# A two-block fp32 transformer kernel on one core: 128-column first weights, a moved memory projection, and a final norm that shares the feed-forward's space

## The chip, the core and the metric

The kernel runs on one core of one Trainium2 chip. The metric is the device time of one execution in microseconds (us), the median of three runs.

## The reference

One sequence of 256 tokens with 1024 features passes two blocks. What matters here:

```python
h = rmsnorm(x, norm_mix[layer])              # x * rsqrt(mean(x*x) + eps) * gain
mix = nsa_attention(h, ...)                  # layer 0; its projections are h @ w_in
x = x + mix
x = x + swiglu(rmsnorm(x, norm_ffn[layer]), ffn_w_up[layer], ffn_w_down[layer])
...                                          # layer 1: dilated attention, then the same swiglu
x = rmsnorm(x, final_norm)                   # end of the first block
...
x = x + 0.5 * swiglu_ffn(rms_norm(x, ffn1_norm[l]), ffn1_w_in[l], ffn1_w_out[l])
mem_kv = rms_norm(mem, mem_norm[l]) @ w_mem_kv[l]      # needs no x at all
...                                          # three-branch mixer, ffn2
x = rms_norm(x, final_norm[l])
```

Inside `nsa_attention` the keys and values of 32-token windows are "compressed": 16 shifted copies of the projected k and v, plus a position term, go through a two-layer perceptron with gelu.

## The kernel before

Activations are held transposed, as eight tiles `x0` to `x7` of 128 features by 256 tokens. The stages run in the order nsa, ffn0, dil (dilated attention), ffn1, ffn1_2 (the first feed-forward of the second block, with the first block's final norm folded in), mix, ffn2_2 and the last norm.

Every projection is made in full fp32 accuracy from halves: a weight tile is loaded as `raw` (1 MB, four buffers, SP's queue, L177), ScalarE copies it to a rounded half `wh` (L190) and VectorE makes the rest `wl` (L191); the input is split in the same way into `xh` (ScalarE, L279) and `xl` (VectorE, L280). `mm3` (L226) then issues three matmuls for each of the eight 128-row pieces, wh·xh (L231), wl·xh and wh·xl, so a projection of 128 columns is 24 matmuls of 256 columns. In the order that TensorE runs them, L231, L232 and L233 are the three products of a piece. A weight pair has four buffers (`wsplit`), and PSUM banks go by the tags mm, sc, tr and ov.

A norm is folded into its projection. The projections take x times the gain, not divided by the root mean square; the squares are summed aside (ScalarE L290 to L295 makes them, POOL adds them at L296, TensorE sums over the features at L304, POOL raises to the power -1/2 at L315, TensorE spreads the row over partitions at L327), and the result is multiplied by R = 1/rms when it leaves PSUM. `norm_twice` (L359) does two norms in a row from one set of x, so ffn1_2 can start from the x that ffn1 leaves: `r1` is the first norm's factor, `r2` the second's, made from `ss2` (L379 to L386).

The program is recorded in Python, and a scheduler then sets a fixed order for each engine from priorities: `high_priority(offset=AHEAD)` pulls work forward by 400 steps, `-BEHIND` pushes it back. On the chip each engine runs its list strictly in order, and a wait holds back all that stands behind it.

Three places matter. At the **start**, `nsa` (L527) norms x, projects the window keys and values (`windows`, L567; the first two weight tiles, `first`, are loaded in `body` with x), and starts the compression (`hidden`, L603, and `compression`, L609, whose gelu is at L613). In the **middle**, `body` calls `mem_project` (L1085) between ffn1 and ffn1_2: four projections of the memory, which need nothing of x. `between` (L1370) is called by `ffn` (L392) before its third and fifth pair of hidden tiles and does `mem_keys` and `s5_prepare`, small VectorE work. At the **end**, `final` (L854) opens a pool of its own for the eight results `res`, scales x by the gain into them (L866), and multiplies by the norm's factor (L874, L876) before the output transfers.

Of the kernel before, what the change touches and what calls it, by code (L numbers as in the profile page):

```python
# [11 lines left out]
F32 = mybir.dt.float32  # L12
F32R = mybir.dt.float32r
AF = mybir.ActivationFunctionType
ALU = mybir.AluOpType
# [3 lines left out]
P = 128  # L19
S = 256  # L20
D = 1024
# [3 lines left out]
EPS = 1e-6  # L25
BIG = 1e30
AHEAD = 400
BEHIND = 100
GAP = 20
WARM = 16  # L30
NU = 384
# [92 lines left out]
class Builder:  # L124
# [221 lines left out]
    def norm_all(self, xs, gains, split=False):  # L346
# [9 lines left out]
            R, r = self.rstd(acc, split)  # L356
        return X, R, r

    def norm_twice(self, pool, xs, first, second):  # L359

        nc = self.nc
        gg = pool.tile([P, KD], F32, name="gg")
        o1, o2 = VOFF[first], VOFF[second]
        nc.vector.tensor_tensor(gg, self.gains[:, o1:o1 + KD], self.gains[:, o2:o2 + KD], ALU.mult)
        acc, acc2 = self.sq_begin(), pool.tile([P, 2, S], F32, name="sqacc2")
        X = []
        with self.tc.high_priority(offset=AHEAD):  # L370
            for k in range(KD):
                X.append(self.gsplit(xs[k], gg[:, k:k + 1], k))
                self.sq_add(acc, xs[k], k)
                self.sq_add(acc2, xs[k], k, self.gain(first, k))
            ps = self.bank("ov")
            self.sq_sum(ps, acc)
            self.sq_sum(ps[:, 2:4], acc2)
            ss2 = pool.tile([P, 2], F32, name="ss2")
            nc.vector.tensor_copy(ss2, ps[:, 2:4])  # L379
            r1 = self.rms(ps[:, 0:2])  # L380
            for _ in range(2):
                for tb in range(2):
                    nc.vector.tensor_tensor(ss2[:, tb:tb + 1], ss2[:, tb:tb + 1], r1[tb], ALU.mult)
            r2 = self.rms(ss2)
            for tb in range(2):
                nc.vector.tensor_tensor(r2[tb], r2[tb], r1[tb], ALU.mult)  # L386
            R = self.rows_kept(r2)
        self.scale(xs, first, self.rows(r1))
        return X, R


    def ffn(self, xs, gain, w_up, w_down, factor, between=None, after=None, skew=0, split=False):  # L392
        nc, tc = self.nc, self.tc
        with tc.tile_pool(name=self.n("hid"), bufs=1) as hp:
            if skew:
                self.pad(hp, skew)
            if after:
                X, R = self.norm_twice(hp, xs, after, gain)
            else:
                (X,), R, _ = self.norm_all(xs, [gain], split)  # L400
            H = []
            self.hid = hp
            for mp in range(KF // 2):
                if mp in (2, 4) and between:
                    between(mp)
                ua = self.units(w_up, D, mp * 256)
                ub = self.units(w_up, D, FF + mp * 256)
                for c in range(2):
                    k = 2 * mp + c
                    pa = self.proj(next(ua), X)  # L410
                    pb = self.proj(next(ub), X)
                    a = hp.tile([P, S], F32, tag="fa", name=self.n("fa"), bufs=2)
                    nc.vector.tensor_tensor(a, pa, R, ALU.mult)
                    b = hp.tile([P, S], F32, tag="fb", name=self.n("fb"), bufs=2)
                    nc.vector.tensor_tensor(b, pb, R, ALU.mult)
                    nc.scalar.activation(a, a, AF.Silu)
                    nc.vector.tensor_tensor(b, a, b, ALU.mult)
                    h = hp.tile([P, S], F32R, name=self.n("hh"), tag=f"hh{k}")
                    l = hp.tile([P, S], F32R, name=self.n("hl"), tag=f"hl{k}")
                    nc.scalar.activation(h, b, AF.Copy)  # L420
                    nc.vector.tensor_tensor(l, b, h.bitcast(F32), ALU.subtract)
                    H.append((h, l))
            self.out_proj(xs, w_down, FF, H, factor)

    def out_proj(self, xs, w, K, X, factor):
        nc = self.nc
# [100 lines left out]
    def nsa(self, xs, first):  # L527
        nc, tc, A = self.nc, self.tc, self.A
        w = A["a_w_in"]
        ukc = itertools.chain(*first)  # L530
        (X,), R, r = self.norm_all(xs, ["norm_mix0"], True)
        with tc.high_priority(offset=-BEHIND):
            self.bias_rows()
        with ExitStack() as es:
# [29 lines left out]

            blks, kcs = [], []

            def windows(wi, units):  # L567
                nm = "kv"[wi]
                if wi == 0:
                    kcs.append(cp.tile([P, 2, 2, S], F32, name="kcv", tag="kcv"))  # L570
                kc = kcs[0][:, wi]
                for mt, u in enumerate(units):
                    self.evac_k(kc[:, mt, :], self.proj(u, X), R)
                blk = cp.tile([P, 16, 60], F32, name="blk" + nm)
                blks.append(blk)
                for gp in range(2):
                    for j2 in range(2):
                        pe = self.v(f"pe_{nm}{j2}", 16)[64 * gp:64 * gp + 64]
                        for half in range(2):
                            src = kc[64 * gp:64 * gp + 64, :, 16 * half:16 * half + 240]  # L580
                            src = src.rearrange("p m (n c j) -> p j c m n", c=8, j=2)[:, j2]
                            dst = blk[64 * j2:64 * j2 + 64, 8 * half:8 * half + 8, 30 * gp:30 * gp + 30]
                            dst = dst.rearrange("p c (m n) -> p c m n", m=2)
                            pb = pe[:, 8 * half:8 * half + 8].unsqueeze(2).unsqueeze(3).to_broadcast([64, 8, 2, 15])
                            (nc.vector if half else nc.gpsimd).tensor_tensor(dst, src, pb, ALU.add)
# [139 lines left out]
                nc.tensor.matmul(Op, Vc[:, g, 2 * j:2 * j + 2, :].rearrange("p i d -> p (i d)"), st["pc"], start=False, stop=True, skip_group_check=True)  # L725
                O.append(self.split_act(Op, "o", 2 * g + j, flip=True))

            windows(0, ukc)
            windows(1, self.units(w, D, 1280))
            keys(0, self.units(w, D, 1536))  # L730
            queries(0)
            keys(1, self.units(w, D, 2048))
# [121 lines left out]
    def final(self, xs, gain):  # L854

        nc = self.nc
        acc = self.sq_begin()
        pool = self.ctx.enter_context(self.tc.tile_pool(name="res", bufs=1))
        res = [pool.tile([P, S], F32, name=f"res{k}") for k in range(KD)]
        Rs = pool.tile([P, S], F32, name="Rs")  # L860
        v = pool.tile([P, 2], F32, name="fv")
        r = pool.tile([P, 2], F32, name="fr")
        with self.tc.high_priority(offset=AHEAD):
            for k in range(KD):
                self.sq_add(acc, xs[k], k, split=True)
# [11 lines left out]
        return res[2:] + res[:2], [*range(2, KD), 0, 1]  # L877

    def scale(self, xs, gain, R):
        for k in range(KD):  # L880
# [458 lines left out]
def body(tc, A, out, stages=None):  # L1339
    stages = stages or STAGES  # L1340
    with ExitStack() as ctx:
        b = Builder(ctx, tc, A)
        nc = b.nc
        xs, first, order = [], [], range(KD)
# [6 lines left out]
        b.rest()  # L1351
        if "nsa" not in stages:
            b.bias_rows()
        late = None
        for s in stages:
# [7 lines left out]
                b.dilated(xs)  # L1363
            elif s == "ffn1":
                b.ffn(xs, "norm_ffn1", A["ffn_w_up1"], A["ffn_w_down1"], 1.0, lambda mp: b.mem_norm(late, mp), skew=352)
                b.mem_project(late)
            elif s == "fin1" and "ffn1_2" not in stages:
                b.final(xs, "final_norm")
            elif s == "ffn1_2":
                def between(mp):  # L1370
                    if mp == 4:
                        return
                    b.vec2 = b.hid.tile([P, 640], F32, name="vec2")[:, :NVEC - NSOON]
                    nc.sync.dma_start(b.vec2, A["vec"][:, NSOON:])
                    b.mem_keys(late)
                    b.s5_prepare(late)
                b.ffn(xs, "ffn1_norm_2", A["ffn1_w_in_2"], A["ffn1_w_out_2"], 0.5, between, "final_norm" if "fin1" in stages else None, skew=288)
            elif s == "mix":
                b.mixer(xs)
            elif s == "ffn2_2":  # L1380
                b.ffn(xs, "ffn2_norm_2", A["ffn2_w_in_2"], A["ffn2_w_out_2"], 0.5, skew=352, split=True)
            elif s == "fin2":
                xs, order = b.final(xs, "final_norm_2")
        for i, (k, x) in enumerate(zip(order, xs)):
            (nc.scalar if i % 2 else nc.sync).dma_start(out[k * P:(k + 1) * P, :], x)


def _pack(I):
# [74 lines left out]
```

## Time and profile before

| what | value |
|---|---|
| three runs | 1338.96, 1335.37 and 1334.37 us |
| median | 1335.37 us |
| profiled execution | 1339.51 us, of which 1337.7 us is the span |
| granted TensorE clock, mean | 0.994 of full |
| busy share of the span | TensorE 98%, VectorE 74%, ScalarE 56%, POOL 15% |

The profiled execution stands 4.14 us above the median. The span is the time from its first to its last instruction on the chip, and 1.8 us of the execution lies around it. TensorE is busy nearly all the time, so what can be won lies in the few places where it is not, or where it runs at the lower of its two clock levels.

### The profile page before, as it was taken

What the parts mean: (1) busy time and instruction counts of PE and PEld (TensorE: products, weight loads), DVE (VectorE), ACT (ScalarE), POOL (GpSimd) and SP (SyncE); (2) the same over time, 40 slices, a digit from 0 to 9 for tenths busy, and PEclk for the clock granted to TensorE, in tenths of its full rate; (3) what the DMA queues carried; (4) which work ended last, traced back from release to release, by engine and by line L of the source; (5) the groups of instructions that cost most, each with busy time, mean ns of one, the idle gap of its engine ahead of it and who ended that gap; (6) DMA issues with size and microseconds to landing.
All of it is one profiled execution on the core that took longest, in us unless ns stands there. A gap on an engine that the chain in (4) does not pass through costs nothing.

```text
span 1337.7 us, 27509 instructions
## 1 busy us (share of the span) xinstructions
PE 1310.3 (98%) x10924; PEld 1245.5 (93%) x10924; DVE 996.5 (74%) x2105; ACT 748.2 (56%) x1422; POOL 196.7 (15%) x244
## 2 busy tenths in 40 slices
PE   9899999999999999999999999999999999999996
PEld 8786999999999887999999999999988879999996
DVE  7899677766797663886855998956699887777752
ACT  5678555555668776754545454544334665555542
POOL 3300100001310000400011332101032044000011
PEclk9999999999999999999999999999999999999998
DMA  9742266646866350665557466755744254566460
GB/s 285 250 151 72 94 205 199 197 144 209 248 204 185 100 143 9 208 195 190 182 174 243 136 200 208 242 180 170 245 154 149 80 174 158 192 196 199 162 198 32
DMA packets 227264, 232.77 MB, mean 174 GB/s; under 512 B 5960, under 2 KB 221328, under 8 KB 227136
## 3 DMA queue, kind: packets, MB, share of 16 engines
q1 hardware_dynamic: 222960, 225.62, 53.0%
q10 hardware_dynamic: 4176, 5.40, 1.2%
q8 instruction: 86, 1.41, 0.4%
q14 instruction: 42, 0.34, 0.1%
HBM read 226.69 MB, written 4.30 MB: 173 GB/s over the span
## 4 chain that ended last, share of the span: by engine, by line
PE 55%; DVE 5%; DMA 1%; issue 1%; ACT 1%; POOL 0%; DVEq 0%; POOLq 0%; ACTq 0%
PE mm L231 7%; PE mm L232 7%; PE mm L233 7%; PE tr L231 4%; PE tr L233 4%; PE tr L232 4%; PE sc L232 4%; PE sc L231 4%; PE sc L233 4%; PE ov L233 2%; PE ov L231 2%; PE ov L232 2%; DVE wl L191 2%; PE ov L493 1%; DMA rot_scratch<-CS 1%
## 5 line engine op out<-in xcount | busy, mean ns | idle before, releaser
L190 ACT ACTIVATE wh<-raw 128x1024 fp32r<-128x1024 f32 (+2 forms) x405 | 417.8, 1036 | 422.9 <-PE mm L232 132.5
L191 DVE TENSOR_TENSOR wl<-raw,wh 128x1024 fp32r<-128x1024 f32 (+2 forms) x405 | 485.1, 1201 | 161.3 <-ACT wh L190 156.8
L231 PE MATMUL mm<-xh,wh 128*128 128x256 f32 x952 | 270.8, 284 | 0.0
L232 PE MATMUL mm<-xl,wh 128*128 128x256 f32 x952 | 267.7, 281 | 1.0 <-DVE xl L280 1.0
L233 PE MATMUL mm<-xh,wl 128*128 128x256 f32 x952 | 267.1, 281 | 1.1 <-DVE wl L191 1.1
L231 PEld LDWEIGHTS mm<-xh,wh 128*128 128x128 f32 x952 | 179.4, 188 | 6.2 <-issue 4.7
L232 PEld LDWEIGHTS mm<-xl,wh 128*128 128x128 f32 x952 | 179.4, 188 | 5.7 <-issue 3.7
L233 PEld LDWEIGHTS mm<-xh,wl 128*128 128x128 f32 x952 | 179.1, 188 | 3.2 <-issue 1.5
L296 POOL TENSOR_TENSOR sqacc<-sqacc,sq 128x256 f32<-128x256 f32 x60 | 57.0, 953 | 536.5 <-ACT sq L295 272.0
L233 PE MATMUL sc<-xh,wl 128*128 128x256 f32 x464 | 129.6, 279 | 0.0
L231 PE MATMUL sc<-xh,wh 128*128 128x256 f32 x464 | 129.5, 279 | 0.0
L232 PE MATMUL sc<-xl,wh 128*128 128x256 f32 x464 | 129.5, 279 | 0.0
L233 PE MATMUL tr<-xh,wl 128*128 128x256 f32 x440 | 123.0, 280 | 3.5 <-DVE wl L191 3.5
L231 PE MATMUL tr<-xh,wh 128*128 128x256 f32 x440 | 123.0, 280 | 0.0
L232 PE MATMUL tr<-xl,wh 128*128 128x256 f32 x440 | 122.8, 279 | 0.0
L233 PEld LDWEIGHTS sc<-xh,wl 128*128 128x128 f32 x464 | 88.0, 190 | 0.1
L231 PEld LDWEIGHTS sc<-xh,wh 128*128 128x128 f32 x464 | 88.0, 190 | 0.0
L232 PEld LDWEIGHTS sc<-xl,wh 128*128 128x128 f32 x464 | 87.9, 189 | 0.0
L233 PEld LDWEIGHTS tr<-xh,wl 128*128 128x128 f32 x440 | 83.5, 190 | 3.9 <-DVE wl L191 3.9
L231 PEld LDWEIGHTS tr<-xh,wh 128*128 128x128 f32 x440 | 83.5, 190 | 0.1
L232 PEld LDWEIGHTS tr<-xl,wh 128*128 128x128 f32 x440 | 83.4, 189 | 0.1
L233 PE MATMUL ov<-xh,wl 128*128 128x256 f32 x224 | 62.2, 278 | 0.2 <-DVE wl L191 0.2
(483 smaller groups left out, 3395.5 us busy)
## 6 DMA issues: line engine op xcount, KB each, us to landing
raw<-in_ffn_w_up_dram SPq DMA_DIRECT2D x44, 1024.0 KB, 5.4
raw<-in_ffn_w_in_dram SPq DMA_DIRECT2D x44, 1024.0 KB, 5.3
raw<-in_w_in_dram SPq DMA_DIRECT2D x17, 1024.0 KB, 5.3
raw<-in_ffn_w_down_dram SPq DMA_DIRECT2D x16, 1024.0 KB, 5.2
raw<-in_ffn_w_out_dram SPq DMA_DIRECT2D x16, 1024.0 KB, 5.1
raw<-in_b_w_q_dram SPq DMA_DIRECT2D x12, 1024.0 KB, 5.2
raw<-in_a_w_in_dram SPq DMA_DIRECT2D x8, 1024.0 KB, 8.3
bt<-u_scratch SPq DMA_DIRECT2D x28, 256.0 KB, 4.7
```

The source lines that it names most:

```text
L190: nc.scalar.activation(hv, v, AF.Copy)
L191: nc.vector.tensor_tensor(lv, v, hv.bitcast(F32), ALU.subtract)
L231: nc.tensor.matmul(ps, sh, mh, start=(i == 0), stop=False)
L232: nc.tensor.matmul(ps, sh, ml, start=False, stop=False)
L233: nc.tensor.matmul(ps, sl, mh, start=False, stop=(i == n - 1))
L296: nc.gpsimd.tensor_tensor(acc[:, 0], acc[:, 0], s, ALU.add)
L493: nc.tensor.matmul(O[64 * i:64 * i + 64, q0:q1], V[kb], pt[:, c0:c0 + q1 - q0], start=(start and kb == 0), stop=(stop and kb == 1), skip_g ...
```

## The change

At the start, the value windows' weights are loaded like the key windows', as 128-column tiles, right behind x; `rest()` (constants and small vectors) moves behind them. All eight x are split first, and the squares are made only then: `norm_begin` gives the squares a scale `one` that is computed from the last `xl`. The four window projections are recorded ahead of the norm's factor, and held in PSUM until it is there. `BEHIND` grows from 100 to 400, which is used for the position-bias rows.

In the middle, `mem_project` moves from ahead of ffn1_2 to its third pair of hidden tiles, and `mem_keys`, `s5_prepare` and their load to the fifth. `norm_twice` hands back its last steps, and `ffn` records them between the first projections.

At the end, `final` runs inside the last feed-forward's pool and takes its tiles from there, and the output transfers are issued in it.

```diff
-BEHIND = 100
+BEHIND = 400
...
+    def norm_begin(self, xs, gain):
+        acc, X = self.sq_begin(), []
+        with self.tc.high_priority(offset=AHEAD):
+            for k in range(KD):
+                X.append(self.gsplit(xs[k], self.gain(gain, k), k))
+            one = self.tmp.tile([P, 1], F32, tag="rv0", name=self.n("one"))
+            self.nc.vector.tensor_scalar(one, X[-1][1].bitcast(F32)[:, 0:1], 1.0, 1.0, ALU.max, ALU.min)
+        for k in range(KD):
+            self.sq_add(acc, xs[k], k, one, True)
+        return X, acc
...
-            R = self.rows_kept(r2)
-        self.scale(xs, first, self.rows(r1))
-        return X, R
+        R = self.tmp.tile([P, S], F32, tag="R", name=self.n("R"))
+        ps, R1 = self.bank("ov")[:, :S], pool.tile([P, S], F32, name="R1")
+        def spread(tb):
+            self.row(ps, r2, tb)
+            nc.vector.tensor_copy(R[:, tb * P:tb * P + P], ps[:, tb * P:tb * P + P])
+        def norm(tb):
+            bk = self.take()
+            self.row(bk, r1, tb)
+            nc.vector.tensor_copy(R1[:, tb * P:tb * P + P], bk[:, tb * P:tb * P + P])
+            if tb == 1:
+                self.scale(xs, first, R1)
+        return X, R, [spread, spread, norm, norm]
...
+                    if steps and mp < 3:
+                        if c == 0:
+                            prods = [self.proj(next(ua), X), self.proj(next(ub), X)]
+                            if mp < 2:
+                                steps[2 * mp](0)
+                            prods.append(self.proj(next(ua), X))
+                            if mp != 1:
+                                steps[mp + 1](1)
+                            prods.append(self.proj(next(ub), X))
+                        pa, pb = prods[2 * c:2 * c + 2]
...
             self.out_proj(xs, w_down, FF, H, factor)
+            return end and end()
...
-        ukc = itertools.chain(*first)
-        (X,), R, r = self.norm_all(xs, ["norm_mix0"], True)
+        uv = itertools.chain(*[self.ahead(self.units(w, D, 1280 + P * i, P)) for i in range(2)])
+        self.rest()
+        X, acc = self.norm_begin(xs, "norm_mix0")
+        KV = [[self.proj(u, X) for u in us] for us in (itertools.chain(*first), uv)]
+        R, r = self.rstd(acc, True)
...
-        pool = self.ctx.enter_context(self.tc.tile_pool(name="res", bufs=1))
+        pool = self.hid
...
                 b.ffn(xs, "norm_ffn1", A["ffn_w_up1"], A["ffn_w_down1"], 1.0, lambda mp: b.mem_norm(late, mp), skew=352)
-                b.mem_project(late)
...
                 def between(mp):
-                    if mp == 4:
+                    if mp == 2:
+                        b.mem_project(late)
                         return
```

**TensorE, from ffn1 to ffn1_2.** Before, behind the last matmul of ffn1 (`mm_9542`) stand the memory's projections; `xh_7599` and `xl_7600` are halves of the memory:

```order
L232 MATMUL mm_9542<-hl_8595,wh_9538 128x256
...
L231 MATMUL sc_9618<-xh_7599,wh_9613 128x256
L232 MATMUL sc_9618<-xl_7600,wh_9613 128x256
L233 MATMUL sc_9618<-xh_7599,wl_9614 128x256
L231 MATMUL sc_9618<-xh_7606,wh_9613 128x256
L232 MATMUL sc_9618<-xl_7607,wh_9613 128x256
```

Now the first four projections of ffn1_2 (`sc_9738`, `tr_9769`, `mm_9800`, `sc_9831`) stand there, taken piece by piece; `xh_9624`, `xl_9625` are the halves of x0, and `xl_9691` that of x7:

```order
L233 MATMUL mm_9546<-hh_8946,wl_9543 128x256
L231 MATMUL sc_9738<-xh_9624,wh_9734 128x256 [waits Activation_49]
L231 MATMUL tr_9769<-xh_9624,wh_9765 128x256
L231 MATMUL mm_9800<-xh_9624,wh_9796 128x256
L231 MATMUL sc_9831<-xh_9624,wh_9827 128x256
L232 MATMUL sc_9738<-xl_9625,wh_9734 128x256 [waits DVE_49]
...
L232 MATMUL sc_9738<-xl_9681,wh_9734 128x256 [waits DVE_49]
L233 MATMUL sc_9738<-xh_9680,wl_9735 128x256
L231 MATMUL sc_9738<-xh_9690,wh_9734 128x256 [waits Activation_49]
L233 MATMUL tr_9769<-xh_9660,wl_9766 128x256
L232 MATMUL sc_9738<-xl_9691,wh_9734 128x256 [waits DVE_49]
L233 MATMUL sc_9738<-xh_9690,wl_9735 128x256
```

The 96 matmuls of the four projections wait for eight `xh` and eight `xl` of x in turn; 58 of them stand ahead of the one that needs the last `xl`, 38 behind. A fifth projection (`tr_9882`, 24 matmuls) follows, and then the spreading of the two norm factors, `r1` (`rr_9709`) and `r2` (`rr_9721`), with two of the memory's matmuls between:

```order
L233 MATMUL tr_9882<-xh_9690,wl_9879 128x256
L327 MATMUL mm_9938<-con,rr_9709 128x128 [waits Pool_49]
L231 MATMUL mm_10026<-xh_7603,wh_10021 128x256 [waits DVE_49,Activation_49]
L232 MATMUL mm_10026<-xl_7604,wh_10021 128x256
L327 MATMUL ov_9730<-con,rr_9721 128x128 [waits DVE_49]
L231 MATMUL ov_9913<-xh_9624,wh_9909 128x256 [waits PE_49]
```

**ScalarE, at the end.** `x_164` is x7, the last tile that the last feed-forward finishes, `x_162` is x6. Before:

```order
L295 ACTIVATE sq_17335<-x_162 128x256
L866 ACTIVATE res_17302<-x_140,gains 128x256
L866 ACTIVATE res_17303<-x_142,gains 128x256
...
L866 ACTIVATE res_17308<-x_162,gains 128x256
L292 ACTIVATE sqacc_17298<-x_164 128x256
L866 ACTIVATE res_17309<-x_164,gains 128x256
```

Now:

```order
L908 ACTIVATE res_17311<-x_160,gains 128x256
L190 ACTIVATE wh_17229<-raw_17141 128x1024
L190 ACTIVATE wh_17233<-raw_17143 128x768
L295 ACTIVATE sq_17339<-x_162 128x256
L908 ACTIVATE res_17312<-x_162,gains 128x256
L292 ACTIVATE sqacc_17305<-x_164 128x256
L908 ACTIVATE res_17313<-x_164,gains 128x256
```

Seven scalings that stood in one block ahead of the last square now stand between the weight copies, each behind its own x.

**ScalarE, in the compression of the start.** `h` is the gelu output of the compression, `z` an exponential of the window attention. Before, both gelus stood together, behind all eight exponentials; now:

```order
L655 ACT_TABLE_LOAD
L655 ACTIVATE h_787<-ov_639 60x256
L716 ACT_TABLE_LOAD
L716 ACTIVATE z_737,den_638<-z_737,mst_637 128x256
L655 ACT_TABLE_LOAD
L655 ACTIVATE h_787<-ov_639 60x256
L716 ACT_TABLE_LOAD
L716 ACTIVATE z_742,den_638<-z_742,mst_637 128x256
```

Two exponentials stand between and behind the gelus, and the program has 11 table loads where it had 9.

## Rows read from the trace of the kernel before

**Rows 1.** The page: the span, and busy time by engine.

```profile
span 1337.7 us, 27509 instructions
...
PE 1310.3 (98%) x10924; PEld 1245.5 (93%) x10924; DVE 996.5 (74%) x2105; ACT 748.2 (56%) x1422; POOL 196.7 (15%) x244
```

**Rows 2.** Windows, start: stretch, length, busy by engine (instructions), TensorE clock, DMA share, GB/s.

```profile
7.60:13.10 5.50, 4.48 (x29) 3.59 (x29) 5.50 (x9) 4.71 (x13) 3.30 (x4) 1.00 1.13 344
13.10:20.00 6.90, 6.90 (x39) 5.66 (x38) 4.09 (x8) 3.20 (x4) 1.08 (x2) 0.75 1.09 295
20.00:30.00 10.00, 10.00 (x90) 10.00 (x89) 9.58 (x17) 4.30 (x5) 3.25 (x4) 1.00 1.08 332
30.00:40.00 10.00, 8.91 (x78) 8.71 (x77) 9.85 (x13) 4.14 (x9) 7.68 (x13) 1.00 0.42 126
```

**Rows 3.** DMA, 1.5 to 31 us: busy tenths in 40 slices.

```profile
DMA  3998999999999999999999999999999999998999
```

**Rows 4.** Timeline of TensorE, start: start, us, instruction.

```profile
18.18 0.81 PE L448 MATMUL tr<-oh,rbt 32*16 32x384 f32 x2
```

**Rows 5.** Timeline of ScalarE, then TensorE, at the compression; in brackets idle time before, releaser.

```profile
60.21 1.06 ACT L190 ACTIVATE wh<-raw 128x1024 fp32r<-128x1024 f32 x1 [3.31 <-DMA raw<-in_a_w_in_dram]
61.29 1.28 ACT L613 ACT_TABLE_LOAD   x1
62.58 0.77 ACT L613 ACTIVATE h<-ov 60x256 f32<-60x256 f32 x2
...
63.41 0.44 PE L616 MATMUL tr<-con,h 128*128 128x128 f32 x2 [1.16 <-ACT h L613]
```

**Rows 6.** Windows, middle.

```profile
730.00:741.00 11.00, 11.00 (x98) 10.82 (x96) 10.48 (x23) 10.46 (x22) 8.38 (x11) 1.00 0.55 182
741.00:748.00 7.00, 4.04 (x22) 4.02 (x22) 7.00 (x16) 1.59 (x3) 1.11 (x2) 0.76 0.01 2
```

**Rows 7.** Timeline of TensorE, middle.

```profile
729.75 0.28 PE L231 MATMUL sc<-xh,wh 128*128 128x256 f32 x1
...
740.51 0.28 PE L233 MATMUL sc<-wh,xl 128*128 128x256 f32 x1
...
743.98 0.38 PE L233 MATMUL tr<-xh,wl 128*128 128x256 f32 x1 [2.96 <-DVE wl L191]
```

**Rows 8.** Timeline of ScalarE, then VectorE, middle.

```profile
731.20 3.30 ACT L279 ACTIVATE xh<-x,gg 128x256 fp32r<-128x256 f32 x8
...
732.07 1.85 DVE L280 SCALAR_TENSOR_TENSOR xl<-x,gg,xh 128x256 fp32r<-128x256 f32 x2
...
734.54 0.47 DVE L280 SCALAR_TENSOR_TENSOR xl<-x,gg,xh 128x256 fp32r<-128x256 f32 x1
...
734.93 0.41 DVE L1090 TENSOR_TENSOR mk<-sc,Rm 128x256 f32<-128x256 f32 x1
...
740.50 1.89 DVE L280 SCALAR_TENSOR_TENSOR xl<-x,gg,xh 128x256 fp32r<-128x256 f32 x2
...
742.72 1.21 DVE L191 TENSOR_TENSOR wl<-raw,wh 128x1024 fp32r<-128x1024 f32 x1
...
749.31 0.16 DVE L379 COPY ss<-ov 128x2 f32<-128x2 f32 x1
...
752.88 0.16 DVE L386 TENSOR_TENSOR rr<-rr,rr 128x1 f32<-128x1 f32 x1
```

**Rows 9.** Timeline, end.

```profile
1324.43 2.90 ACT L866 ACTIVATE res<-x,gains 128x256 f32<-128x256 f32 x7 [6.77 <-PE tr L233]
1324.43 0.43 DVE L431 SCALAR_TENSOR_TENSOR x<-tr,x 128x256 f32<-128x256 f32 x1 [7.28 <-PE tr L233]
1327.24 0.40 ACT L292 ACTIVATE sqacc<-x 128x256 f32<-128x256 f32 x1
```

**Rows 10.** Windows, end.

```profile
1324.30:1332.00 7.70, 2.53 (x11) 2.05 (x10) 0.90 (x3) 3.99 (x10) 0.98 (x2) 0.74 0.00 0
```

More of the change, by code (lines that the diff above doesn't have):

```diff
@@ L386, in norm_twice, with ffn @@
                 nc.vector.tensor_tensor(r2[tb], r2[tb], r1[tb], ALU.mult)
-            R = self.rows_kept(r2)
-        self.scale(xs, first, self.rows(r1))
-        return X, R
-    def ffn(self, xs, gain, w_up, w_down, factor, between=None, after=None, skew=0, split=False):
+        R = self.tmp.tile([P, S], F32, tag="R", name=self.n("R"))
[10 more added lines that the diff above has]
+        return X, R, [spread, spread, norm, norm]
+    def ffn(self, xs, gain, w_up, w_down, factor, between=None, after=None, skew=0, split=False, end=None):
         nc, tc = self.nc, self.tc
@@ L397, in ffn @@
             if after:
-                X, R = self.norm_twice(hp, xs, after, gain)
+                X, R, steps = self.norm_twice(hp, xs, after, gain)
             else:
                 (X,), R, _ = self.norm_all(xs, [gain], split)
+                steps = []
             H = []
@@ L407, in ffn @@
                 ub = self.units(w_up, D, FF + mp * 256)
+                prods = []
                 for c in range(2):
                     k = 2 * mp + c
-                    pa = self.proj(next(ua), X)
-                    pb = self.proj(next(ub), X)
+                    if steps and mp < 3:
[8 more added lines that the diff above has]
+                        pa, pb = prods[2 * c:2 * c + 2]
+                    else:
+                        pa = self.proj(next(ua), X)
+                        pb = self.proj(next(ub), X)
                     a = hp.tile([P, S], F32, tag="fa", name=self.n("fa"), bufs=2)
@@ L565, in nsa, with windows @@
             blks, kcs = [], []
-            def windows(wi, units):
+            def windows(wi):
                 nm = "kv"[wi]
@@ L571, in windows @@
                 kc = kcs[0][:, wi]
-                for mt, u in enumerate(units):
-                    self.evac_k(kc[:, mt, :], self.proj(u, X), R)
+                for mt, p in enumerate(KV[wi]):
+                    self.evac_k(kc[:, mt, :], p, R)
                 blk = cp.tile([P, 16, 60], F32, name="blk" + nm)
@@ L726, in values @@
                 O.append(self.split_act(Op, "o", 2 * g + j, flip=True))
-            windows(0, ukc)
-            windows(1, self.units(w, D, 1280))
+            windows(0)
+            windows(1)
             keys(0, self.units(w, D, 1536))
@@ L876, in final @@
                 nc.vector.tensor_tensor(res[k], res[k], R, ALU.mult)
-        return res[2:] + res[:2], [*range(2, KD), 0, 1]
+        return [(k, res[k]) for k in (*range(2, KD), 0, 1)]
     def scale(self, xs, gain, R):
@@ L1343, in body @@
         nc = b.nc
-        xs, first, order = [], [], range(KD)
+        xs, first = [], []
         for k in range(KD):
@@ L1350, in body @@
                 first.append(b.ahead(b.units(A["a_w_in"], D, 1024 + P * (k // 4), P, 4)))
-        b.rest()
         if "nsa" not in stages:
+            b.rest()
             b.bias_rows()
@@ L1380, in body, with end @@
             elif s == "ffn2_2":
-                b.ffn(xs, "ffn2_norm_2", A["ffn2_w_in_2"], A["ffn2_w_out_2"], 0.5, skew=352, split=True)
+                def end():
+                    order = b.final(xs, "final_norm_2")
+                    for i, (k, x) in enumerate(order):
+                        (nc.scalar if i % 2 else nc.sync).dma_start(out[k * P:(k + 1) * P, :], x)
+                b.ffn(xs, "ffn2_norm_2", A["ffn2_w_in_2"], A["ffn2_w_out_2"], 0.5, skew=352, split=True, end=end)
             elif s == "fin2":
-                xs, order = b.final(xs, "final_norm_2")
-        for i, (k, x) in enumerate(zip(order, xs)):
-            (nc.scalar if i % 2 else nc.sync).dma_start(out[k * P:(k + 1) * P, :], x)
+                pass
 def _pack(I):
```

## The prediction

> **What bounds the kernel now.** I read the page first, for which engine carries the span. TensorE is busy 1310.3 us of 1337.7 [rows 1], so 27.4 us of idle time, and what runs at the lower clock, is all that a change without fewer matmuls can reach. Then I cut out the three stretches that the change touches with the windows view, and in each asked who ends TensorE's waits. At the start two things are full at once: the DMA engines, at nine tenths or more in nearly every slice from 1.5 to 31 us [rows 3], and VectorE, 9.58 and 9.85 of 10 us between 20 and 40 us [rows 2]. In the middle TensorE works through from 730 to 741 us, then gets 4.04 of 7 us with a mean clock of 0.76 [rows 6]: the timeline shows one wait of 2.96 us for a `wl` [rows 7], after which TensorE stays for a while at the lower of its levels, 1.2 GHz. At the end ScalarE works off seven `res` before the last square [rows 9].
>
> **The start: 0 us, between -3.6 and +2.6.** The change takes away waits of TensorE: 5.50 - 4.48 = 1.02 us for the first inputs, (1 - 0.75) x 6.9 = 1.73 us lost to the lower clock behind them [rows 2], and 0.81 us of bias rows that move back [rows 4], together 3.6 us; the four window projections will be done that much earlier, or more. But they are not what is late afterwards. The same megabytes must come in over DMA engines that are already full to 31 us, and the order of weights against small inputs moves bytes about without removing any; and VectorE has the same weight splits and window copies to make while it is 96 to 98% busy [rows 2]. What is late next is the `wl` of the key projections, so TensorE, done sooner with the window projections, waits longer for them. I take 0; the end at -3.6 is the case that all of it comes through, should VectorE, whose first `xl` run without POOL beside them, begin its list that much sooner. One `one` on a [128, 1] column is hidden in that list. The other end is the compression: two more table loads of 1.28 us [rows 5] are 2.6 us on ScalarE, and the gelu there is waited for already (1.16 us, [rows 5]); I leave them at 0 in the sum because the weight copy ahead of the first load waits 3.31 us for its transfer [rows 5], so a gelu that no longer waits behind that has room.
>
> In the trace of before the load is followed at once by the gelu (61.29 + 1.28 = 62.57, start 62.58) [rows 5]. The Trainium skill, ScalarE: Activation LUTs, section What ACT_TABLE_LOAD costs, adds a drain of about 1380 ns to the 1283 ns of the load; by it the upper end would be 2 x 2.66 = 5.3 us, an estimate, and the row does not bear it out.
>
> **The middle: +3.9 us, between -2.4 and +9.4.** Before, the 96 matmuls of the memory run from 729.75 to 740.51 us, one every 10.76 / 95 = 0.1133 us [rows 7], and cover the making of `xh` and `xl`. The change takes this cover away: the next four projections, again 96 matmuls, now need x itself. Without a wait they would be through at 729.75 + 96 x 0.1133 = 740.6. But the first `xh` starts at 731.20 and takes about half a us [rows 8], so TensorE stands for 1.95 us at once. Then it follows VectorE. The eight `xl` begin at 732.07, and the last pair starts at 740.50 and ends 1.89 us later, at 742.39 [rows 8]: they stand among small work of `s5_prepare`, whose order there is almost the same after the change, and most take about 0.95 us, where one takes 0.47 [rows 8]. I leave out one `mk` of 0.41 us [rows 8], which goes with the memory, so the last `xl` comes at 741.98. Of the 96 matmuls 38 stand behind it: 741.98 + 38 x 0.1133 = 746.3, 5.7 us late (the 1.95 included).
>
> The fifth projection ends at 746.3 + 24 x 0.1133 = 749.0. Behind it stands the spreading of `r2`, which before had its cover too. Its chain from `ss` to the product took 749.31 to 753.04, 3.7 us [rows 8], with one `wl` of 1.2 us in it. Now `ss` can be read from about 745.5, ahead of the end of the fourth projection, which gives 749.2: no wait, if no other weight split gets in between, and 2.4 us if two do [rows 8]. In VectorE's new order one more stands ahead, so I take 1.2 us. The lower clock I take as before, since the wait is no shorter: (1 - 0.76) x 7 = 1.7 us [rows 6]. Lost after: 5.7 + 1.2 + 1.7 = 8.6. Lost before, in the same stretch: 2.96 + 1.7 = 4.7 [rows 6, 7]. The difference is +3.9. The memory's projections themselves only move, into a stage where weights are split at the pace that TensorE needs; the cover for `mem_keys` and `s5_prepare` is the rest of that feed-forward, several hundred matmuls, and I cost them at nothing.
>
> **The end: -2.4 us, between -3.2 and -2.0.** x7 is written at 1324.43 + 0.43 = 1324.86, and its square starts only at 1327.24, behind seven `res` of 2.90 us that all waited for the last matmul, though their x had been ready long before [rows 9]: the pool of `res` takes over space that the hidden tiles held to the end. From the hidden tiles' own pool they need not wait, and their new places, between weight copies, are on an engine that is busy 56% [rows 1]. So the square starts 2.4 us sooner. The gap may also spare part of the lower clock in the tail (0.74 there, [rows 10]), which sets the further end; the nearer one is a square that waits for x6's scaling, 0.4 us.
>
> **The sum.** 0 + 3.9 - 2.4 = +1.5, so the profiled execution of 1339.5 becomes 1341.0; it stands 4.1 us above the median, which gives 1336.9 us. With the start's two ends and a middle between +2 and +5.5, the likeliest case alone spans 1332 to 1341.
>
> **The rivals.** 1. *The `xl` keep ahead.* If the other `xl` take 0.47 us like the one at 734.54 [rows 8], each is done before the 12 matmuls of a piece (1.36 us) are through; TensorE then waits for the first pair only, 732.07 + 0.47 - 729.75 less four matmuls = 2.3 us, its clock does not fall, and `r2` is in time. The middle gives 2.3 - 4.7 = -2.4, the end -2.4, the start half of its 3.6: 1335.4 - 6.6 = 1328.8. For it: VectorE has two split weights less to make behind them. Against: POOL is busy 8.38 of the 11 us [rows 6] with the same sums of squares, and the squares follow the `xh` as before.
>
> 2. *The start comes through.* The sum with -3.6 in the first place: 1333.3. For it, VectorE's 4.09 of 6.9 us from 13 to 20 us [rows 2], which an earlier norm could fill; against it, rows 3.
>
> 3. *The clock stays down in the middle: slower.* In the 12.2 us from 729.75 to 741.98 TensorE gets 58 matmuls, 6.6 us of work in pieces of three to twelve, where before it worked through. One wait of 2.96 us was enough for the fall seen in rows 6. If the clock falls in the first 1.95 us and the pieces do not bring it back, a matmul costs 0.227 us, a piece of twelve 2.7 us, more than an `xl`, and TensorE itself becomes the bound: 731.7 + 96 x 0.227 = 753.5 instead of 746.3 and 1.7 of slow clock, +5.5, and 1342.4 in all. It decides if the granted clock is 0.5 over more than half of that stretch.
>
> The Trainium skill, TensorE: Matmul & The Clock Gate, section What's actually happening, speaks for this one: the lower level is the default and sustained activity is what lifts it. The rows agree that the clock comes back only some time after the matmuls do; that a half-busy stretch keeps it down, no row of before shows.
>
> **How the numbers follow.** The forecast has 0.37, rival 1 0.27, rival 2 0.12, rival 3 0.24. A difference under 0.3%, 4.0 us, is one that a measurement of this kernel can hardly tell from none: faster means under 1331.4, slower above 1339.4. Rival 1 is faster, with a little from rival 2: 0.30. Rival 3 is slower, with the upper tail of the forecast (table loads on the path): 0.28. The rest is 0.42. The range takes in rivals 1 and 3 at their values: 1328.5 to 1342.5.
>
> **What would show it.** Right: waits of TensorE `<- DVE xl` between 732 and 742 us that sum to over 3 us, none for the `wl` behind the memory; TensorE at the hidden-layer matmuls of the compression at the same time as before though the window projections end some 4 us sooner; the last square within 0.3 us of x7. Wrong: `xl` of 0.5 us in a row, or window projections whose lead is still there at 64 us.

## The result, and the profile after

The changed kernel takes 1350.97 us in the median of four runs (1348.68 to 1352.46), the kernel before 1334.98: a ratio of 1.0107, with a 95% interval of 1.0087 to 1.0128, so about 14 us slower, where I forecast 1336.9. The ratio is not the quotient of the two medians, which lie 16.0 us apart; all differences below go by the ratios. The profiled executions are 1348.68 us after and 1339.51 us before, which is the slowest one of before; they show 9 us of the loss.

The page of the changed kernel, span and busy time:

```profile
span 1346.9 us, 27506 instructions
...
PE 1311.8 (97%) x10924; PEld 1241.0 (92%) x10924; DVE 997.2 (74%) x2108; ACT 753.0 (56%) x1424; POOL 193.4 (14%) x244
```

Busy time is what it was [rows 1]: nothing was added, TensorE waits longer. To see where, I set the starts of the updates of x that end a stage's projections side by side in the two traces. These are the last of nsa and the first of ffn1_2, before:

```profile
163.82 0.41 DVE L431 SCALAR_TENSOR_TENSOR x<-tr,x 128x256 f32<-128x256 f32 x1
...
881.28 0.42 DVE L431 SCALAR_TENSOR_TENSOR x<-mm,x 128x256 f32<-128x256 f32 x1 [0.34 <-PE mm L233]
```

After:

```profile
174.54 0.41 DVE L469 SCALAR_TENSOR_TENSOR x<-tr,x 128x256 f32<-128x256 f32 x1
...
896.99 0.42 DVE L469 SCALAR_TENSOR_TENSOR x<-tr,x 128x256 f32<-128x256 f32 x1 [0.25 <-PE tr L233]
```

At the end of nsa the changed kernel is 10.7 us late, at the end of ffn1 10.4, at the first x of ffn1_2 15.7 and at its last 13.7, at x7 ahead of the last norm 12.6, and at the end of the span 9.2. So the start costs 10.7, the middle 5.3, and the end gives 3.4 back; the 2.0 us between first and last x of ffn1_2 come back where nothing was changed (last section). The middle and the end are near my forecast; the start, which I took as 0, is the loss.

The windows of the start, changed kernel (stretch, length, busy by engine, clock, DMA share, GB/s):

```profile
7.60:13.10 5.50, 4.90 (x35) 4.41 (x35) 4.63 (x10) 4.71 (x10) 0.00 (x0) 1.00 1.17 301
13.10:20.00 6.90, 6.58 (x57) 6.38 (x56) 3.13 (x3) 6.08 (x12) 5.08 (x6) 1.00 1.13 281
20.00:30.00 10.00, 9.73 (x74) 8.13 (x72) 7.78 (x13) 4.25 (x5) 2.60 (x3) 1.00 0.99 307
30.00:40.00 10.00, 8.94 (x75) 8.76 (x75) 9.90 (x15) 1.79 (x3) 8.04 (x8) 1.00 0.56 175
40.00:50.00 10.00, 6.83 (x36) 4.69 (x37) 9.72 (x17) 6.83 (x15) 5.66 (x12) 0.88 0.82 257
```

Against [rows 2] it begins well: TensorE has 4.90 us in the first stretch instead of 4.48, and there is no lower clock from 13 to 20 us. But VectorE, the engine that I held to be full, has 3.13 of 6.9 us (before 4.09) and 7.78 of 10 (9.58). That share alone does not show the loss: by the profile VectorE waits there for `wh`, which ScalarE makes as weights land (2.16 us ahead of 25.05 us), and a version without any loss (e10 below) has 6.99 of the same 10 us. What comes late stands in the timelines. Before (three rows of POOL, TensorE and VectorE):

```profile
8.58 3.58 POOL L296 TENSOR_TENSOR sqacc<-sqacc,sq 128x256 f32<-128x256 f32 x4 [1.81 <-ACT sq L295]
...
13.08 1.00 PE L304 MATMUL ov<-ones,sqacc 128*128 128x1 f32 x8
...
25.71 0.42 DVE L496 TENSOR_TENSOR kcv<-mm,R 128x256 f32<-128x256 f32 x1
```

After (ScalarE, POOL, TensorE, VectorE):

```profile
13.55 0.49 ACT L290 ACTIVATE sqacc<-x,one 128x256 f32<-128x256 f32 x1
...
14.52 7.00 POOL L296 TENSOR_TENSOR sqacc<-sqacc,sq 128x256 f32<-128x256 f32 x6 [13.16 <-ACT sq L295]
...
21.58 1.05 PE L304 MATMUL ov<-ones,sqacc 128*128 128x1 f32 x8 [0.27 <-POOL sqacc L296]
...
30.72 0.41 DVE L534 TENSOR_TENSOR kcv<-mm,R 128x256 f32<-128x256 f32 x1
```

The squares start at 13.55 us, behind the last split of x and a weight copy; POOL's six sums then take 7.00 us (before, two ran from 5.24 us and the four shown behind them), and the sum over features (L304) comes at 21.58 instead of 13.08. The window copies `kcv`, which need the norm's factor, stand at 30.72 instead of 25.71, and with them all that VectorE has behind them. From 40 to 50 us TensorE gets 6.83 us, where before it got 8.83.

The second piece is the compression (ScalarE, then TensorE; before in [rows 5]):

```profile
62.88 1.06 ACT L190 ACTIVATE wh<-raw 128x1024 fp32r<-128x1024 f32 x1 [0.23 <-PE sc L704]
63.96 1.28 ACT L655 ACT_TABLE_LOAD   x1
65.25 0.38 ACT L655 ACTIVATE h<-ov 60x256 f32<-60x256 f32 x1
65.64 1.28 ACT L716 ACT_TABLE_LOAD   x1
67.53 1.28 ACT L655 ACT_TABLE_LOAD   x1
68.83 0.38 ACT L655 ACTIVATE h<-ov 60x256 f32<-60x256 f32 x1
69.26 0.44 PE L658 MATMUL tr<-con,h 128*128 128x128 f32 x2 [2.76 <-ACT h L655]
```

The two gelus are 3.6 us apart with two table loads between, and TensorE waits 2.76 us where it waited 1.16. Its matmul on `h` starts at 69.26 us, before at 63.41 [rows 5]: 5.85 of the 10.7 us are lost up to here, and 4.9 in the attention behind it.

In the middle, the waits of TensorE (for what: us in total, times, longest) and the windows:

```profile
PE sc L231 <- ACT xh L279: 1.8, 1, 1.8
PE mm L231 <- DVE CS L1053: 1.6, 1, 1.6
PE sc L232 <- DVE xl L280: 1.0, 2, 0.6
PE sc L231 <- DVE fa L450: 0.8, 1, 0.8
```

```profile
740.40:751.40 11.00, 8.19 (x50) 7.68 (x51) 10.55 (x21) 7.88 (x18) 9.61 (x12) 0.84 0.68 216
751.40:770.00 18.60, 16.83 (x128) 16.28 (x127) 16.75 (x100) 6.75 (x8) 4.51 (x11) 0.91 0.36 115
```

The one wait of 2.96 us for a `wl` [rows 7] is gone, and waits for `xh`, for VectorE ahead of the memory's projection, for `xl` and for a result tile have come in its place; the clock falls as before, 3.4 us long, and a second time around 765 us. At the end, the last square follows x7 at once:

```profile
1337.01 0.42 DVE L469 SCALAR_TENSOR_TENSOR x<-sc,x 128x256 f32<-128x256 f32 x1 [7.28 <-PE sc L233]
1337.46 0.42 ACT L292 ACTIVATE sqacc<-x 128x256 f32<-128x256 f32 x1 [6.83 <-DVE x L469]
1337.79 0.49 ACT L908 ACTIVATE res<-x,gains 128x256 f32<-128x256 f32 x1
```

x7 is written at 1337.01 + 0.42 = 1337.43 us, and the square starts at 1337.46, where it waited 2.4 us before [rows 9]; none of the seven `res` stands between them any more, and the one behind is x7's own.

### The profile page after: what moved, and what is told of

Its sections match the earlier page's. It is cut to its first block, busy times and chain, and to the rows that moved or that the text cites. A ratio compares the mean times of both kernels' runs of the same rounds, so it can differ in the third digit from the quotient of the medians.

```text
span 1346.9 us, 27506 instructions
## 1 busy us (share of the span) xinstructions
PE 1311.8 (97%) x10924; PEld 1241.0 (92%) x10924; DVE 997.2 (74%) x2108; ACT 753.0 (56%) x1424; POOL 193.4 (14%) x244
## 4 chain that ended last, share of the span: by engine, by line
PE 56%; DVE 5%; issue 1%; ACT 1%; DMA 0%; POOL 0%; DVEq 0%; ACTq 0%; POOLq 0%
PE mm L231 7%; PE mm L232 7%; PE mm L233 7%; PE tr L231 4%; PE tr L233 4%; PE tr L232 4%; PE sc L231 4%; PE sc L233 4%; PE sc L232 4%; PE ov L231 2%; PE ov L232 2%; PE ov L233 2%; DVE wl L191 2%; PE ov L531 1%; PE ov L1104 1%
## 5 line engine op out<-in xcount | busy, mean ns | idle before, releaser
L296 POOL TENSOR_TENSOR sqacc<-sqacc,sq 128x256 f32<-128x256 f32 x60 | 60.5, 1013 | 555.7 <-ACT sq L295 291.0
L233 PE MATMUL tr<-xh,wl 128*128 128x256 f32 x432 | 120.2, 278 | 0.0
L231 PE MATMUL tr<-xh,wh 128*128 128x256 f32 x432 | 120.1, 278 | 0.0
L232 PE MATMUL tr<-xl,wh 128*128 128x256 f32 x432 | 120.1, 278 | 0.0
L231 PE MATMUL ov<-xh,wh 128*128 128x256 f32 x224 | 63.4, 283 | 0.0
```

The source lines that it names most:

```text
L231: nc.tensor.matmul(ps, sh, mh, start=(i == 0), stop=False)
L232: nc.tensor.matmul(ps, sh, ml, start=False, stop=False)
L233: nc.tensor.matmul(ps, sl, mh, start=False, stop=(i == n - 1))
L296: nc.gpsimd.tensor_tensor(acc[:, 0], acc[:, 0], s, ALU.add)
```

## The experiments

All ratios are to the kernel before, with 95% intervals; 0.001 is 1.3 us. First the three parts by themselves.

**e1: the start alone** (`norm_begin`, the loads, the four projections ahead, `BEHIND` 400; the rest as before).

> The kernel before with the start of the change alone. Theory A, the late norm: the squares, held back until x is split, make the norm's factor some 4 to 8 us late, the window copies wait for it on VectorE and everything behind them; then this alone is 8 to 13 us slower than before, and the profile shows the first kcv at about 30.7 us as in the changed kernel (25.7 before). Rival B, the start is neutral as I forecast and the lag in the changed kernel's start is a chance of that one run: within 3 us of before. Rival C, the loss comes from how the three parts meet: the sum of the three single parts is clearly under the 16 us of the whole.

Measured 1.0093 (1.0072 to 1.0115), +12.4 us. Theory A's size, and rival B is out. With e3 and e4 the parts sum to 12.4 + 3.9 - 2.4 = 13.9 us, against 14.3 for the whole: no sign that they meet in a bad way (rival C), as far as the intervals, some 4.5 us together, can tell.

**e2: the start with early squares.** Against e1; the squares also move into the block of raised priority.

```diff
-            one = self.tmp.tile([P, 1], F32, tag="rv0", name=self.n("one"))
-            self.nc.vector.tensor_scalar(one, X[-1][1].bitcast(F32)[:, 0:1], 1.0, 1.0, ALU.max, ALU.min)
-        for k in range(KD):
-            self.sq_add(acc, xs[k], k, one, True)
+            for k in range(KD):
+                self.sq_add(acc, xs[k], k, split=True)
```

> The start of the change alone, but with the squares made between the splits as before, and no scale from the last xl; 128-column weights, small inputs behind them, four projections ahead of the factor and the bias rows pushed back all stay. Theory A: the lag goes, kcv stands at 25 us or sooner and the time is from 4 us faster than before to 2 us slower. Rival D, the order of the loads is what makes the start late (con, vec and the key weights come later): the lag stays, 6 us or more slower than before.

Measured 1.0037 (1.0023 to 1.0050), +4.9 us. The loss shrinks by 7.5 us, as theory A wants, but not to nothing. The profile (VectorE, then TensorE) shows a new wait:

```profile
23.10 0.42 DVE L506 TENSOR_TENSOR kcv<-mm,R 128x256 f32<-128x256 f32 x1
...
33.04 1.94 DVE L461 SCALAR_TENSOR_TENSOR u<-tr,um 16x384 f32<-16x384 f32 x4
...
35.03 0.58 PE L231 MATMUL tr<-xh,wh 128*128 128x256 f32 x1 [4.39 <-DVE u L461]
```

`kcv` comes 2.6 us sooner than before. But the bias rows, pushed back by `BEHIND`, leave their PSUM bank only when VectorE copies them (`u`) at 33.04, behind the window copies, and TensorE, whose next projection needs that bank, stands for 4.39 us. So the wait that this version shows is neither for late loads nor for the norm, but for a bank.

**e3: the middle alone.**

> The kernel before with the moved memory projection and the deferred norm steps alone. My forecast for this part was +3.9 us by waits for xh and xl between 730 and 742 us; in the trace of the changed kernel the lag grows by 5.3 us to the first output tile of ffn1_2 and by 3.4 us over the whole stage. Expected: 3 to 6 us slower. Rival, the cover is not needed and the lag of the changed kernel comes from its earlier start: within 1.5 us of before.

Measured 1.0029 (1.0018 to 1.0041), +3.9 us, what I had forecast for it. Its waits, with the start as before (TensorE, 728 to 860 us), and the clock:

```profile
PE sc L231 <- ACT xh L279: 1.8, 1, 1.8
PE mm L231 <- DVE CS L1036: 1.7, 1, 1.7
PE ov L1015 <- ACT bt L1017: 1.3, 1, 1.3
PE sc L232 <- DVE xl L280: 1.0, 3, 0.5
PE sc L231 <- DVE fa L438: 0.9, 1, 0.9
```

```profile
731.00:734.40 3.40, 3.11 (x15) 2.81 (x15) 3.39 (x11) 3.37 (x10) 3.24 (x4) 0.51 1.03 354
```

**e4: the end alone.**

> The kernel before with the final norm's tiles in the hidden tiles' pool alone. Expected: the last square follows x7 at once, 2.4 to 3.4 us faster than before, less than 0.3%. Rival, the tail is bound by something else (output transfers): no change in the tail's length.

Measured 0.9982 (0.9970 to 0.9994), -2.4 us, as forecast.

Then the start in pieces.

**e5: the start with the bias rows as before**, that is, `BEHIND = 100` and all else of the start.

> The start of the change alone with BEHIND left at 100: squares still held back, bias rows less far back, and 9 table loads instead of 11. If the late norm carries the loss (theory A), this stays 6 to 10 us slower than before; the table loads (2.6 us, and a wait of 2.8 us for the gelu in the changed kernel) and the late bias rows are the rest, so 3 to 5 us under the 12.4 us of the start alone. If the table loads and the bias rows carry it (rival E), it falls to within 4 us of before.

Measured 1.0025 (1.0013 to 1.0038), +3.3 us. A miss for theory A, which wanted 6 to 10, and in the range of rival E: one constant takes 9 of the 12.4 us away, though the squares are as late (`kcv` at 32.07 us) and VectorE's copies with them. With the constant the gelus stand together again, so the table loads are in the 9 us. The late norm is part of the loss, and the order that the scheduler makes of it is the larger part.

**e6: early squares and `BEHIND = 100`.**

> The start of the change alone with early squares and BEHIND at 100. What is left of the change is the 128-column loads ahead, small inputs behind them, and four projections ahead of the factor. The early squares alone left 4.9 us over before. If the bias rows, pushed back, made them (rival F: they keep VectorE from the weight splits at 33 to 36 us), this is from 3 us faster to 1 us slower than before; if the order of the loads makes them (rival D), it stays 3 us or more slower.

Measured 1.0015 (1.0004 to 1.0026), +2.0 us, between the two ranges. Less than either alone, but not nothing: the wait for the bank is still there (4.0 us on `u`), since at 100 the rows still fall behind the window copies. Beside e5, held-back squares add 1.3 us at 100; beside e2 and e1 they add 7.5 at 400. The two edits act on each other.

**e7: late squares in the kernel before**, nothing else.

```diff
-        (X,), R, r = self.norm_all(xs, ["norm_mix0"], True)
+        acc, X = self.sq_begin(), []
+        with self.tc.high_priority(offset=AHEAD):
+            for k in range(KD):
+                X.append(self.gsplit(xs[k], self.gain("norm_mix0", k), k))
+            one = self.tmp.tile([P, 1], F32, tag="rv0", name=self.n("one"))
+            nc.vector.tensor_scalar(one, X[-1][1].bitcast(F32)[:, 0:1], 1.0, 1.0, ALU.max, ALU.min)
+            for k in range(KD):
+                self.sq_add(acc, xs[k], k, one, True)
+            R, r = self.rstd(acc, True)
```

> The kernel before with one thing changed: the squares of the first norm take their scale from the last xl, so that they come behind all splits. Loads, projections and bias rows are as before. Theory A: the factor is 4 to 8 us late, the window copies with it, and the time is 5 to 9 us above before. Rival C (it only hurts together with the new loads): within 2 us of before.

Measured 1.0061 (1.0042 to 1.0079), +8.1 us: held-back squares alone are enough for a loss of theory A's size. Here TensorE itself waits for POOL's sums, and then works at the lower of its clock levels (window row, clock 0.51):

```profile
PE ov L304 <- POOL sqacc L296: 5.4, 1, 5.4
```

```profile
20.00:30.00 10.00, 6.50 (x30) 6.50 (x31) 4.21 (x7) 0.99 (x2) 6.28 (x8) 0.51 0.96 284
```

`kcv` comes at 36.10 us, later than in e1 (31.18). The changed kernel has neither that wait (0.27 us) nor that clock (1.00 from 20 to 30 us), so e7 prices late squares by themselves and not the path by which they cost the changed kernel. Beside e5 (+3.3, squares held back as well, POOL's sums done at 20.8 us against 23.4) it suggests what the early projections do: they cover about 5 us of what the late squares make TensorE wait. Where the squares are early there is no such wait to cover.

**e9: the two gelus together**, in the start alone. The order of TensorE, VectorE, POOL and SP is e1's row by row; ScalarE has two table loads less.

```diff
-                for i in range(2):
-                    nc.scalar.activation(h1[64 * i:64 * i + 60], hb[64 * i:64 * i + 60, :256], AF.Gelu_apprx_tanh)
+                with self.tc.high_priority(offset=120):
+                    for i in range(2):
+                        nc.scalar.activation(h1[64 * i:64 * i + 60], hb[64 * i:64 * i + 60, :256], AF.Gelu_apprx_tanh)
```

> The start of the change alone, with the two gelus of the compression given a higher priority, which puts them side by side again: 9 table loads instead of 11, the order of TensorE, VectorE, POOL and SP the same row by row. Two loads of 1.28 us and the exponential between are 3.1 us between the weight copy and the second gelu, and the changed kernel waits 2.8 us for it. Theory A2 (the loads are on the path): 2.5 to 3.1 us under the start alone, so about 9 to 10 us over before. Rival: another wait takes its place (the attention behind it is bound by VectorE), under 1 us.

Measured 1.0055 (1.0032 to 1.0078), +7.3 us: 5 us less than e1, but the two intervals overlap, and together they leave some 1 to 9 us (an estimate, their half-widths added as squares). The traces say more. In e1 TensorE waits 2.75 us for the second gelu, in e9 not at all, and its matmul on `h` starts at 66.63 us instead of 69.92, 3.3 us sooner, where the five traces with the old start lie within 1.1 us. So the loads are on the path up to there. At the end of nsa 1.6 us of it are left: e9 needs 1.7 us more for the stretch between.

The rest against e5 (+3.3) comes in that stretch, the attention: `h` is used at 66.63 us in e9 and at 66.93 in e5, and at the end of nsa e9 is 6.5 us later. TensorE in that stretch, e9 and then e5:

```profile
66.63:173.79 107.16, 101.07 (x776) 83.86 (x774) 86.17 (x310) 72.80 (x204) 10.11 (x20) 0.98 0.33 105
```

```profile
66.93:167.28 100.35, 97.78 (x774) 82.67 (x774) 84.49 (x300) 71.91 (x200) 11.54 (x20) 1.00 0.35 113
```

TensorE is idle for 6.1 us in e9 and for 2.6 in e5; the longest waits of e9 are

```profile
PE sc L679 <- DVE mst L688: 1.4, 2, 1.1
PE ov L742 <- DVE pc L722: 0.8, 1, 0.8
```

From 106.4 to 112 us no matmul of a projection stands between the heads' scores in e9, where e5 has 13; TensorE stands for 1.9 us there while the scores wait for VectorE, in e5 not at all. The idle time makes 3.5 us; a clock of 0.83 between 70 and 80 us in e9, where e5 has 1.00, is 1.7 more. The rest of the 6.8, some 1.6 us, I did not find.

**e10: early squares, bias rows not pushed back** (`BEHIND = 0`).

> The start with early squares and the bias rows not pushed back at all (BEHIND 0). With early squares, the profile shows kcv at 23.1 us, 2.6 us sooner than before, but then TensorE waits 4.4 us for the copies u of the bias rows, which hold a PSUM bank and stand on VectorE behind the window copies. Without that wait (u ahead of kcv again): 1 to 4 us faster than before if the early loads are worth anything; within 1 us of before if VectorE and the transfers bind the start, as I forecast.

Measured 0.9999 (0.9983 to 1.0015). VectorE now copies `u` ahead of `kcv`:

```profile
17.99 1.94 DVE L461 SCALAR_TENSOR_TENSOR u<-tr,um 16x384 f32<-16x384 f32 x4 [0.74 <-PE tr L458]
...
27.36 0.42 DVE L506 TENSOR_TENSOR kcv<-mm,R 128x256 f32<-128x256 f32 x1
```

The wait for the bank is gone, and so is the loss; a gain there is not. `kcv` comes at 27.36 us, later than before (25.71), and nsa ends as before (table below). With everything harmful taken out, the early loads are neutral. Held-back squares with `BEHIND = 0` were not tried.

The traces bear on all of these. Before, e3, e4, e8 and e11 share the old start, and their update of the last x of nsa starts at 163.01 to 164.08 us, 163.6 in the mean; their matmul on `h` at 62.66 to 63.73, 63.2 in the mean; and 100.3 to 100.4 us lie between. Against those means, beside what the ratio gives (us):

| | e1 | e2 | e5 | e6 | e7 | e9 | e10 |
|---|---|---|---|---|---|---|---|
| matmul on `h` | +6.7 | +1.9 | +3.7 | +4.0 | +8.1 | +3.4 | -0.4 |
| from there to the last x | +5.1 | -0.6 | 0.0 | -0.6 | 0.0 | +6.8 | +0.5 |
| last x of nsa | +11.8 | +1.3 | +3.7 | +3.4 | +8.1 | +10.2 | +0.1 |
| by the ratio | +12.4 | +4.9 | +3.3 | +2.0 | +8.1 | +7.3 | -0.1 |

Five agree within 1.4 us, so the loss is made before the end of nsa. The attention behind the compression is longer only where held-back squares and `BEHIND = 400` meet, in e1 and e9 (and in the changed kernel, +4.9); the late norm by itself and the table loads cost ahead of it. In e9 the trace shows 2.9 us more than the ratio, which I did not explain. In e2 it shows 3.6 us less: the wait for the bank is there, but most of it is won back before nsa ends, and 2.0 us of what comes later in that execution is the slower passage of the last section. What the bank costs is thus open between 1 and 5 us.

Last, what can be kept.

**e8: the middle with the cover.** Deferred norm steps, `mem_project` left between the two feed-forwards.

> The middle of the change with the memory's projections left between ffn1 and ffn1_2, only the last steps of the double norm recorded between the first projections. If the loss of the middle (1.0029) is the missing cover, as I forecast, this is within 1.5 us of before, or up to 2 us faster where r2 is no longer waited for. If the deferred steps themselves cost it (rival), it stays 3 us slower.

Measured 0.9993 (0.9981 to 1.0005): the loss of the middle is the missing cover, not the deferred steps.

**e11: the end, and the middle with the cover.**

> The end of the change, and its deferred norm steps with the memory's projections left in their old place; the start as before. By the single runs (0.9982 and 0.9993) 3 us faster than before, between 1 and 5.

Measured 0.9961 (0.9947 to 0.9975), -5.2 us, a little more than expected, and with e12 the fastest version: 1331.82 us in the median. In its middle one wait of TensorE is left, the old one:

```profile
PE tr L233 <- DVE wl L191: 3.0, 1, 3.0
```

**e12: the same with the start of e10.**

> As the last, and with the start of early squares and BEHIND 0. If that start is worth 1 to 4 us, 4 to 7 us faster than before; if it is neutral, 3 us.

Measured 0.9962 (0.9950 to 0.9974): the start adds nothing, as e10 said.

## Why the prediction was wrong

**The start: wrong, and by the whole of the error.** The step that failed is "VectorE has the same weight splits and window copies to make while it is 96 to 98% busy", and from it "I take 0". I read VectorE's busy share as a load that the change would not touch, and asked only whether it could begin sooner. A share says nothing of what the engine waits for next; the norm's factor is such a thing, and I gave the held-back squares no term at all, though the diff holds them back in so many words. Before, the last four of POOL's six sums ended at 12.16 us and the sum over features ran at 13.08; after, all six begin behind the last split and take 7.0 us. e7 gives late squares alone +8.1 us, e5 +3.3 with the projections ahead as cover, and e1, where the bias rows are pushed back as well, +12.4. For the loads themselves the 0 was right (e10, -0.1). What I named as late next, the `wl` of the key projections, was not: TensorE's waits for `wl` from 5 to 60 us are 1.8 us after and 2.3 before. The sign that I gave, the compression's matmul on `h` at the same time as before, missed by 5.85 us.

"I leave them at 0 in the sum because the weight copy ahead of the first load waits 3.31 us for its transfer": the table loads were bounded at 2.6 us and then left out. In the changed kernel that copy waited 0.23 us for TensorE, not for a transfer, so the room was not there; e9 puts the loads on the path, with 3.3 us at the matmul on `h`, of which its trace keeps 1.6 to the end of nsa. I had the added loads in the order's rows and a wait of 1.16 us for the same gelu in the profile, and that wait should have decided. The Trainium skill, ScalarE: Activation LUTs, section What ACT_TABLE_LOAD costs, adds a drain of 1380 ns to each load; here again the gelu follows its load at once (63.96 + 1.28 = 65.24, start 65.25), as it did before, so no drain stands in these rows.

The bias rows I counted as a gain of 0.81 us for moving back. In e2 they held a PSUM bank until VectorE emptied it behind the window copies, and TensorE stood for 4.4 us. In the whole change four of the five copies of `u` stand ahead of the late window copies, and that wait did not show; what the same constant cost there is the longer attention (+4.9 us) and the parted gelus. Why the scheduler's order makes the attention that much longer is explained only in part (e9).

**The middle: right in its cause and in size, the size in part by luck.** Forecast +3.9, e3 measured +3.9 (2.4 to 5.5). By its steps: the wait for the first `xh` was forecast at 1.95 and is 1.8 us. The last `xl` ends at 740.72 + 0.47 = 741.19 in e3, whose ffn1 ends 1.03 us sooner than in the trace of before, so at 742.2 against 741.98. But the waits for `xl` are 1.0 us in all, not 3.7, and under the 3 us that I had named as the sign: TensorE ran at half speed from 731 to 734.4 us (mean 0.51) and did in that time what I had it waiting through. The wait for `r2` that I gave 1.2 us did not come; 1.7 us for VectorE stand two matmuls sooner, ahead of the memory's first, and 1.3 and 0.9 us (`bt`, `fa`) for which I had no term. So the sum came out with other terms in it. That the loss is the missing cover, e8 shows. Rival 1, in which the `xl` keep ahead, did not come; rival 3, a clock that stays low, came for 3.4 us and not for more than half of its 12.2.

**The end: right.** Forecast -2.4, e4 measured -2.4, and the square is 0.03 us behind x7 (1337.46).

**The sum.** +3.9 - 2.4 held; 0 for the start should have been about +12. The range ended at 1342.5, the value of rival 3, which puts its loss in the middle; no rival put one at the start, where rival 2 looked only for a gain and the start's own end stood at +2.6. (By the terms given, the likeliest case begins at 1331.4, not 1332.)

## What to carry to other kernels

A change that delays something small (eight squares) is priced by following what it feeds up to the first engine that has to wait for it, and not by the busy share of that engine: 97% busy is a load only as long as its inputs come in time, and a lower share is not yet a loss (e10). An instruction that is moved back keeps its buffers that much longer, so ask who needs the bank next; and where a scheduler sets the order, one constant can be worth more than the edit beside it (9 of 12 us here, the parted gelus included), so measure the parts apart and each with the old constant. Work that needs nothing of the running result, like the memory's projections here, is worth most where the next stage's input is still being made.

## What the runs showed of the hardware that I had not expected

Whole passages of matmuls run at one of two rates with the granted clock at 1.00 and no wait. The last projection of ffn1_2, kernel before and e10, window rows:

```profile
881.30:936.00 54.70, 54.70 (x467) 54.70 (x466) 32.93 (x36) 26.21 (x36) 6.38 (x7) 1.00 0.58 181
```

```profile
880.80:933.30 52.50, 52.50 (x466) 52.50 (x465) 32.71 (x36) 26.14 (x36) 6.29 (x7) 1.00 0.59 187
```

The same work, 467 and 466 matmuls in the records, takes 54.70 us in one execution (117 ns each) and 52.50 us in the other (113 ns), TensorE busy throughout in both. The profiled execution of before has the slower rate here, which is 2 us of its time; e2, e4 and e8 have it too, 453 matmuls from 881 to 934 us where the nine other experiments and the changed kernel have 470 or 471, and e4 and e8 have the old start and e2 a new one. What sets it was not tried. One profile of each kernel cannot tell whether it belongs to the execution or to the program; in the second case 2 us of the difference between e11 (fast there, -5.2) and its parts e4 and e8 (slow there, together -3.3) would be this passage.
